# Toeplitz tiles of a state-space mixer laid out on chip by sixteen transfers, in place of a write and a windowed read of memory

## The chip, the cores and the metric

One core of a Trainium2 chip runs the kernel. The metric is the time of one execution on the device in microseconds (us), the median of a few runs. The work of a core is done by TensorE (PE: matmuls), VectorE (DVE), ScalarE (ACT), GpSimd (POOL) and the queue of the sync engine (SP), which issues the transfers. Each engine takes its instructions strictly in the order in which they were written; a semaphore holds an instruction, and with it everything behind it on that engine, until what it needs is there.

## The reference

One layer of a decoder with three groups of heads in parallel: a state-space mixer (S5), differential attention, and sliding-window attention. Sequence 1024, width 1024, float32. What the change touches is the state-space mixer:

```
def s5_mixer(u, lam_re, lam_im, log_step, b_re, b_im, c_re, c_im, d_skip, w_glu, b_glu):
    ...
    bu_re = jnp.einsum('bsgh,gph->bsgp', ug, bb_re)
    bu_im = jnp.einsum('bsgh,gph->bsgp', ug, bb_im)
    ...
    _, _, st_re, st_im = lax.associative_scan(combine, (a_re, a_im, bu_re, bu_im), axis=1)
    y = (jnp.einsum('bsgp,ghp->bsgh', st_re, c_re.astype(jnp.float32))
         - jnp.einsum('bsgp,ghp->bsgh', st_im, c_im.astype(jnp.float32))
         + d_skip.astype(jnp.float32).reshape(SSM_GROUPS, SSM_GROUP) * ug)
    y = jax.nn.gelu(y.reshape(bsz, seq, SSM_WIDTH))
    ...
proj = h @ w_in
(u, z_ssm, qd, kd, vd, z_diff, qs, ks, vs, z_swa) = split_cols(proj)
y_ssm = s5_mixer(u, ...) * jax.nn.silu(z_ssm)
...
y = jnp.concatenate([y_ssm, y_diff, y_swa], axis=-1) @ w_out
return rms_norm(x + gate[:, None, :] * y, final_gain)
```

There are 16 groups of 16 channels with a complex diagonal state of 64 each.

## The kernel before

The projections of the columns of `w_in` (tiles `zu1`, `zs0`, `zs1`, `vs`, `ks`, `qs0`, `qs1`, then `z0`, `v0`, `q0`, `k0`, ...) run one after another on PE. Each weight tile `wr_*` is loaded over the sync queue two tiles ahead (`load_w`, called in `next_w`), split one tile ahead into a high part `wh_*` (a copy on ACT) and a low part `wl_*` (a subtraction on DVE or POOL, `split_w`), and multiplied in three products a step, 24 matmuls for each half `p_*0`, `p_*1` of the sequence. An evacuation then takes the bank: for a query tile, `ev_q` (L1176) writes two pages `qs0m0`, `qs0m1` (or `qs1m*`), their high parts by ACT and their low parts by DVE.

Beside this stream runs the state-space mixer. It works in chunks of eight steps: inside a chunk the convolution is a matmul with a lower-triangular block Toeplitz tile `T`, and between chunks a scan carries the state.

- `ssm_small` (L430) makes `AP`, the powers 0 to 8 of the complex step. `ssm_tables` makes `H`, powers times input weights, and from it, by transposes, `E`.
- `ssm_lags` (L623) makes `CA` and, for the two halves m of the groups, the 16 x 16 blocks of `K` for the eight lags: matmuls into `pK`, two ACT copies, the DVE rows `dd` and `K<-K,dd` for the skip term. `K` has 16 partitions. `T` has 128: row block t holds the lags shifted by t. Before, `K` is written behind seven blocks of zeros (from the page `kz`) into a scratch `kscr` in memory, and one read with overlapping windows lays out the tile: partition block i begins 7 - i blocks from the rear.
- `ssm_main` (L1036) loads `U`, the inputs, with sixteen transfers. Row blocks stand in reversed order, which goes with the reversed rows of `T` and with `AP[..., 0:8]` in `H`.
- `ssm_state(m)` makes the chunk states: matmuls into `pV`, DVE products `tg<-pV,PH`, a sum, a scan, and the result `Xs`.
- `ssm_out(q)` (L1106), q = 0 to 3, is a block of 32 short matmuls on PE into a bank `pY`: `T` times `U` and `CA` times `Xs`. It needs `T`, `Xs` and a free bank of the tag `ps`, of which there are two, shared with `pV`. Its GELU follows on ACT and DVE in the tile `gw`.

Three things set the order around the change. First, a cost model (`Model`, L29 to L94) and a mixer (`Mixer`, L168 to L226): side jobs are generators, and after each step of the projection stream `mix.tick()` writes down the next piece of any job whose inputs the model holds to be ready. So a changed cost or transfer shifts the order in which later instructions stand on all engines. In the model a transfer to 16 partitions takes 0.7 on the sync queue and any other 0.47. Second, all queues are in order. Third, the pages: `page()` (L249) gives every tile one of 50 slots of 4 KB by 128 partitions, in a ring, and a slot passes from a tile that is done to a later one. The first writer of the new tile waits for the last reader of the old one. One page more or fewer early on changes who inherits from whom later.

```
    def page(name, shape=(128, 1024), dt=F32):
        return big.tile(list(shape), dt, name=name, tag="pg", bufs=NPG)
```

All instructions are recorded through one helper, so that every row of the profile says L109; rows are told apart by tile.

Of the kernel before, what the change touches and what calls it, by code (L numbers as in the profile page):

```python
# [8 lines left out]
F32 = mybir.dt.float32  # L9
# [220 lines left out]
def body(ctx, tc, x, c, norm_gain, ada_w, ada_b, w_in, w_out, lam_re, lam_im, log_step,  # L230
# [199 lines left out]
    def ssm_small():  # L430

        M = 12582912.0
        t, kf, r, t2 = small("t_"), small("kf"), small("r_"), small("t2")
        ki = cst.tile([128, 8], I32, name="ki")

        def ts(o, i, s1, o1=OP.mult, s2=None, o2=OP.add):
            if s2 is None:
                V.tensor_scalar(o, i, s1, None, op0=o1)
            else:
                V.tensor_scalar(o, i, s1, s2, op0=o1, op1=o2)  # L440
            return ("V",)

        def tt(o, a, b, op=OP.mult):
            V.tensor_tensor(o, a, b, op)
            return ("V",)

        def stt(o, i, s1, b, o1=OP.mult, o2=OP.add):
            V.scalar_tensor_tensor(o, i, s1, b, op0=o1, op1=o2)
            return ("V",)

        def horner(o, x, ks):

            yield ts(o, x, ks[0])
            for k in ks[1:]:
                yield stt(o, o, k, x, OP.add, OP.mult)

        def exp(o, i):
            yield ts(t, i, -87.0, OP.max, 88.0, OP.min)
            yield ts(kf, t, 1.0 / math.log(2.0))
            yield ts(kf, kf, M, OP.add)  # L460
            yield ts(kf, kf, M, OP.subtract)
            yield stt(r, kf, -0.693359375, t)
            yield stt(r, kf, 2.12194440e-4, r)
            yield from horner(o, r, (1.0 / 5040, 1.0 / 720, 1.0 / 120, 1.0 / 24, 1.0 / 6, 0.5, 1.0))
            ts(kf, kf, 127.0, OP.add, 8388608.0, OP.mult)
            V.tensor_copy(ki, kf)
            yield ("V",)
            yield stt(o, o, 1.0, ki.bitcast(F32), OP.add, OP.mult)

        step, x1, mag, ang = small("step"), small("x1"), small("mag"), small("ang")  # L470
        yield from exp(step, ls)
        tt(x1, lr, step)
        yield tt(ang, li, step)
        yield from exp(mag, x1)
        yield ts(t, ang, 2.0 / math.pi)
        yield ts(kf, t, M, OP.add)
        yield ts(kf, kf, M, OP.subtract)
        yield stt(r, kf, -1.5703125, ang)
        for cc in (-4.837512969970703e-4, -7.549789948768648e-8):
            yield stt(r, kf, cc, r)  # L480
        r2, sn, cs = small("r2"), small("sn"), small("cs")
        yield tt(r2, r, r)
        yield from horner(sn, r2, (1.0 / 362880, -1.0 / 5040, 1.0 / 120, -1.0 / 6))
        yield tt(sn, sn, r)
        yield tt(sn, sn, r, OP.add)
        yield from horner(cs, r2, (-1.0 / 3628800, 1.0 / 40320, -1.0 / 720, 1.0 / 24, -0.5))
        yield ts(cs, cs, 1.0, OP.add)
        f1, b0, b1 = small("f1"), small("b0"), small("b1")
        for q, i, b in ((f1, kf, b0), (t, f1, b1)):

            yield ts(q, i, 0.5, OP.mult, -0.25)
            yield ts(q, q, M, OP.add)
            yield ts(q, q, M, OP.subtract)
            yield stt(b, q, -2.0, i)
        yield ts(b1, b1, -2.0, OP.mult, 1.0)
        e = cst.tile([128, 2, 8], F32, name="e")
        yield tt(t2, cs, sn, OP.subtract)
        yield tt(t2, t2, b0)
        yield tt(t2, t2, sn, OP.add)
        yield tt(e[:, 1], t2, b1)  # L500
        yield tt(t2, cs, sn, OP.add)
        yield tt(t2, t2, b0)
        yield tt(t2, cs, t2, OP.subtract)
        yield tt(e[:, 0], t2, b1)
        PW["e"] = e

        AP = page("AP", (128, 2, 8, 9))
        G.memset(AP[:, 0, :, 0:1], 1.0)
        G.memset(AP[:, 1, :, 0:1], 0.0)
        yield tt(AP[:, :, :, 1], e, mag[:, None, :].to_broadcast([128, 2, 8]))  # L510
        pt = page("pt_", (128, 4, 8, 4))
        for n in (1, 2, 4):
            src = [AP[:, u, :, 1:n + 1] for u in range(2)]
            bc = [AP[:, u, :, n:n + 1].to_broadcast([128, 8, n]) for u in range(2)]
            q = [pt[:, j, :, :n] for j in range(4)]
            tt(q[0], src[0], bc[0])
            tt(q[1], src[1], bc[1])
            yield tt(q[2], src[0], bc[1])
            tt(q[3], src[1], bc[0])
            tt(AP[:, 0, :, n + 1:2 * n + 1], q[0], q[1], OP.subtract)  # L520
            yield tt(AP[:, 1, :, n + 1:2 * n + 1], q[2], q[3], OP.add)
        fre, fim, am, t3 = small("fre"), small("fim"), small("am"), small("t3")
        yield ts(am, AP[:, 0, :, 1], 1.0, OP.subtract)
        tt(t2, AP[:, 1, :, 1], li)
        yield tt(fre, am, lr)
        tt(t3, am, li)
        yield tt(fim, AP[:, 1, :, 1], lr)
        tt(fre, fre, t2, OP.add)
        yield tt(fim, fim, t3, OP.subtract)
        tt(fre, fre, den)  # L530
        yield tt(fim, fim, den)
        M8 = small("M8")
        yield tt(M8, mag, mag)
        yield tt(M8, M8, M8)
        yield tt(M8, M8, M8)
        PW.update(AP=AP, M8=M8, fre=fre, fim=fim)

    def ssm_phases():

# [20 lines left out]
    def ssm_tables():  # L560

        yield from ssm_small()
        yield (when(lambda: "B" in PW),)
        AP, fre, fim = PW["AP"], PW["fre"], PW["fim"]
        t0 = page("tb0", (128, 8, 8, 16))
        t1 = page("tb1", (128, 8, 8, 16))
        fb = [f[:, :, None].to_broadcast([128, 8, 16]) for f in (fre, fim)]
        v0, v1 = t0[:, :, 0, :], t1[:, :, 0, :]
        for u in range(2):
            tts(v0, Bq[:, u], fb[0], OP.mult)  # L570
            tts(v1, Bq[:, 1 - u], fb[1], OP.mult)
            tts(BB[:, u], v0, v1, OP.add if u else OP.subtract)
            yield ("V",)
        for u in range(2):
            for g2 in range(2):
                V.tensor_copy(BS[RH[u], :, g2], BB[RH[g2], u])
        mix.add(ssm_lags())
        H = [page(f"H{u}", (128, 8, 8, 16)) for u in range(2)]
        av = [AP[:, u, :, 0:8][:, :, :, None].to_broadcast([128, 8, 8, 16]) for u in range(2)]
        bv = [BB[:, u][:, :, None, :].to_broadcast([128, 8, 8, 16]) for u in range(2)]  # L580
        for u in range(2):
            tts(t0, av[0], bv[u], OP.mult)
            yield ("V",)
            tts(t1, av[1], bv[1 - u], OP.mult)
            yield ("V",)
            tts(H[u], t0, t1, OP.add if u else OP.subtract)
            yield ("V",)

        E = [page(f"E{u}", (128, 8, 128)) for u in range(2)]
        PW["E"] = E  # L590
        for u in range(2):
            for m in range(2):
                yield (H[u], bank("pt"))
                p = pst("pt", "pE", (128, 4, 128))
                for a in range(4):
                    PE.transpose(p[:, a], H[u][:, 4 * m + a].rearrange("p a b -> p (a b)"), ident)
                A.activation(E[u][:, 4 * m:4 * m + 4], p, AF.Copy)
                rel(p)
# [19 lines left out]
                yield (c_,)  # L618
        PW["ph"] = 1

    kscr = [dram.tile([16, 8, 15, 16], F32, name=f"kscr{m}") for m in range(2)]

    def ssm_lags():  # L623
        kz = page("kz", (16, 8, 7, 16))
        G.memset(kz, 0.0)
        for m in range(2):
            SP.dma_start(kscr[m][:, :, 0:7, :], kz)
        yield (Cn, bank("pt"))
        psc = pst("pt", "psc", (128, 2, 128))
        for u in range(2):  # L630
# [32 lines left out]
        rel(pd)  # L663
        Tm = [page(f"T{m}", (128, 8, 8, 16)) for m in range(2)]
        for m in range(2):
            K = page(f"K{m}", (16, 8, 8, 16))
            for g2 in range(2):
                yield (CA[m][g2], BS, bank("pt"))
                p = pst("pt", "pK", (16, 4, 128))
                for a in range(4):  # L670
# [6 lines left out]
            tts(dd, ident[:16, None, :16].to_broadcast([16, 8, 16]),  # L677
                dT[:, 8 * m:8 * m + 8, None].to_broadcast([16, 8, 16]), OP.mult)
            tts(K[:, :, 0, :], K[:, :, 0, :], dd, OP.add)

            SP.dma_start(kscr[m][:, :, 7:15, :], K)
            SP.dma_start(Tm[m].rearrange("p a b c -> p a (b c)"),
                         dap(kscr[m], 0, [[16, 8], [15 * 128, 16], [15 * 16, 8], [1, 128]]))
        PW["T"] = Tm


# [349 lines left out]
    def ssm_main():  # L1036
        Uu = []
        for f in range(2):
            t = page(f"U{f}", (128, 8, 128))
            for tt in range(8):  # L1040
                SP.dma_start(t[112 - tt * 16:128 - tt * 16], dap(uscr, f * 128 * 1024 + tt * 128,
                                                           [[1024, 16], [16 * 1024, 8], [1, 128]]))
            Uu.append(t)
        yield (when(lambda: "ph" in PW and "E" in PW),)
# [633 lines left out]
```

## Time and profile before

| | |
|---|---|
| median of three runs | 572.88 us (569.91 to 575.13) |
| profiled execution | 573.08 us |
| its span, first to last instruction | 571.3 us |
| mean granted clock of PE | 0.991 |
| busy time of PE | 553.9 us of the span |

A row of the timeline gives the start in us, the duration, the engine, the operation, output and inputs with their shapes, how many such instructions are joined, and in brackets how long the engine stood idle before and what released it. A row of the windows gives a stretch, its length, the busy time of PE, of PE's weight loads, DVE, ACT and POOL with their counts, then the clock that PE was granted (1.00 is full), the share of the transfer engines that was busy and GB/s. A row of the waits gives engine and tile, what it waited for, us in total, times and the longest.

### The profile page before, as it was taken

To read this page: it belongs to the slowest core of one execution; us is meant where nothing else is said; L and a number is where in the kernel's file an instruction comes from. 1 tells how busy PE (TensorE), PEld (TensorE's weight loads), DVE (VectorE), ACT (ScalarE), POOL (GpSimd) and SP (SyncE) were. 2 spreads that over 40 slices of the span, in tenths; PEclk is the share of its full clock that TensorE was granted. 3 is DMA by queue.
4 is the path that set the end of the run, shared out by engine and by line. 5 is a ranking of instruction groups with operands and counts; after the bars stand their busy time and mean duration, and the time that the engine had idled before them with its cause. 6 is when DMAs were issued, how large, how long until landed. Compare 5 with 4: busy or idle time off the path is not lost.

```text
span 571.3 us, 9236 instructions
## 1 busy us (share of the span) xinstructions
PE 553.9 (97%) x3170; PEld 464.3 (81%) x3170; DVE 403.8 (71%) x1061; ACT 262.3 (46%) x595; POOL 188.3 (33%) x339
## 2 busy tenths in 40 slices
PE   8999999999997999999999999999999999989995
PEld 6767888888887996777888889998888878878884
DVE  4886886997687666788666777744766867765534
ACT  6545221255142545435555766535575456442211
POOL 3254170000135036442646172323453522120011
PEclk9999999999998999999999999999999999989998
DMA  8993076002712430437320111015026402051411
GB/s 315 353 349 71 3 202 138 0 2 47 148 37 52 86 105 38 176 130 230 103 73 2 38 37 38 2 34 188 2 75 215 154 1 65 0 178 64 139 38 73
DMA packets 60634, 57.12 MB, mean 100 GB/s; under 512 B 11375, under 2 KB 52906, under 8 KB 60586
## 3 DMA queue, kind: packets, MB, share of 16 engines
q1 hardware_dynamic: 60518, 56.50, 32.9%
q8 instruction: 25, 0.41, 0.3%
q14 instruction: 23, 0.19, 0.1%
q10 hardware_dynamic: 68, 0.02, 0.0%
HBM read 46.83 MB, written 9.68 MB: 99 GB/s over the span
## 4 chain that ended last, share of the span: by engine, by line
PE 86%; DVE 9%; ACT 2%; issue 2%; POOLq 0%; POOL 0%; DVEq 0%; ACTq 0%
PE po L109 14%; PE pb L109 10%; PE p_v L109 7%; PE p_k L109 6%; PE p_z L109 6%; PE pS L109 6%; PE pdO L109 6%; PE p_q L109 5%; PE p_zs L109 4%; PE p_qs L109 3%; PE pdT L109 2%; PE p_ks L109 2%; PE p_vs L109 2%; PE p_zu L109 2%; PE pa L109 2%
## 5 line engine op out<-in xcount | busy, mean ns | idle before, releaser
L109 ACT ACTIVATE sp<-sp,dmx 128x128 f32<-128x128 f32 (+7 forms) x64 | 49.0, 768 | 18.4 <-DVE dmx L109 18.3
L109 PE MATMUL po<-woh,yh 128*128 128x512 f32 (+1 forms) x136 | 52.3, 384 | 0.1
L109 PE MATMUL po<-woh,yl 128*128 128x512 f32 (+1 forms) x136 | 51.6, 379 | 0.3 <-DVE yl L109 0.3
L109 PE MATMUL po<-wol,yh 128*128 128x512 f32 (+1 forms) x136 | 51.4, 378 | 0.0
L109 POOL TENSOR_SCALAR dmx<-dmx 128x1 f32<-128x1 f32 x32 | 6.5, 204 | 112.0 <-ACT oo L109 111.2
L109 DVE CUSTOM_DVE_ANT_0 sp<-pS,bd 128x384 f32<-128x384 f32 (+3 forms) x64 | 33.8, 552 | 10.3 <-PE pS L109 9.6
L109 PE MATMUL p_v<-wh_v,hh 128*128 128x256 f32 x128 | 37.8, 295 | 0.0
L109 PE MATMUL p_v<-wl_v,hh 128*128 128x256 f32 x128 | 36.4, 285 | 1.0 <-POOL wl_v L109 1.0
L109 PE MATMUL p_v<-wh_v,hl 128*128 128x256 f32 x128 | 36.2, 283 | 0.0
L109 POOL TENSOR_TENSOR swp<-swp,swm 128x256 f32<-128x256 f32 x30 | 19.9, 696 | 41.0 <-DVE swm L109 31.9
L109 PEld LDWEIGHTS po<-woh,yl 128*128 128x128 f32 x136 | 25.6, 188 | 5.5 <-DVE yl L109 0.7
L109 PEld LDWEIGHTS po<-woh,yh 128*128 128x128 f32 x136 | 25.8, 189 | 4.6 <-ACT yh L109 0.3
L109 ACT ACTIVATE jk<-res 128x512 f32<-128x512 f32 (+1 forms) x16 | 9.8, 616 | 42.3 <-DVE res L109 42.3
L109 PEld LDWEIGHTS po<-wol,yh 128*128 128x128 f32 x136 | 25.7, 189 | 4.2
L109 POOL TENSOR_TENSOR wl_z<-wr_z,wh_z 128x256 fp32r<-128x256 f32 x16 | 12.6, 818 | 44.7 <-ACT wh_z L109 44.7
L109 PE MATMUL p_k<-hh,wh_k 128*128 128x512 f32 x64 | 26.3, 411 | 0.0
L109 PE MATMUL p_q<-hh,wh_q 128*128 128x512 f32 x64 | 26.1, 407 | 0.0
L109 PEld LDWEIGHTS p_v<-wl_v,hh 128*128 128x128 f32 x128 | 24.4, 191 | 1.9 <-POOL wl_v L109 1.4
L109 PE MATMUL p_z<-hh,wh_z 128*128 128x512 f32 x64 | 25.5, 398 | 0.0
L109 PEld LDWEIGHTS p_v<-wh_v,hh 128*128 128x128 f32 x128 | 24.4, 190 | 0.9 <-issue 0.8
L109 PE MATMUL p_q<-hh,wl_q 128*128 128x512 f32 x64 | 25.1, 393 | 0.0
L109 PE MATMUL p_k<-hh,wl_k 128*128 128x512 f32 x64 | 25.1, 393 | 0.0
(486 smaller groups left out, 1673.9 us busy)
## 6 DMA issues: line engine op xcount, KB each, us to landing
aw<-in_ada_w_dram SPq DMA_DIRECT2D x32, 256.0 KB
x<-in_x_dram SPq DMA_DIRECT2D x8, 512.0 KB
gaw<-in_ada_w_dram SPq DMA_DIRECT2D x8, 512.0 KB
wo<-in_w_out_dram SPq DMA_DIRECT2D x8, 512.0 KB
xr<-in_x_dram SPq DMA_DIRECT2D x8, 512.0 KB
out_dram<-res SPq DMA_DIRECT2D x16, 256.0 KB
yt<-ycat SPq DMA_DIRECT2D x48, 64.0 KB
wr_z<-in_w_in_dram SPq DMA_DIRECT2D x4, 512.0 KB
```

Source lines behind the costliest of these rows:

```text
L109: return f(*args, **kw)
```

## The change

Four edits go together.

1. A new page `ARV` holds `AP` in reversed order of the powers, made by eight copies on POOL, and `H` is made from `ARV`. 
2. The scratch `kscr`, the page `kz`, its memset and its two transfers are gone.
3. `T` is set to zero on POOL, two memsets of 1024 elements a partition, and each half m is then laid out by eight transfers from `K` in place: the t-th writes the 16 partitions of row block t with the lags 0 to 7 - t, for 8 groups: for t = 0 a run of 4 KB in each partition, else 8 runs of 448 down to 64 bytes.
4. `U` is loaded with its row blocks in natural order.

```diff
--- before.py
+++ after.py
@@ -519,6 +519,9 @@
             tt(q[3], src[1], bc[0])
             tt(AP[:, 0, :, n + 1:2 * n + 1], q[0], q[1], OP.subtract)
             yield tt(AP[:, 1, :, n + 1:2 * n + 1], q[2], q[3], OP.add)
+        ARV = page("ARV", (128, 2, 8, 8))
+        for j in range(8):
+            G.tensor_copy(ARV[:, :, :, j], AP[:, :, :, 7 - j])
         fre, fim, am, t3 = small("fre"), small("fim"), small("am"), small("t3")
         yield ts(am, AP[:, 0, :, 1], 1.0, OP.subtract)
         tt(t2, AP[:, 1, :, 1], li)
@@ -533,7 +536,7 @@
         yield tt(M8, mag, mag)
         yield tt(M8, M8, M8)
         yield tt(M8, M8, M8)
-        PW.update(AP=AP, M8=M8, fre=fre, fim=fim)
+        PW.update(AP=AP, ARV=ARV, M8=M8, fre=fre, fim=fim)
 
     def ssm_phases():
 
@@ -561,7 +564,7 @@
 
         yield from ssm_small()
         yield (when(lambda: "B" in PW),)
-        AP, fre, fim = PW["AP"], PW["fre"], PW["fim"]
+        ARV, fre, fim = PW["ARV"], PW["fre"], PW["fim"]
         t0 = page("tb0", (128, 8, 8, 16))
         t1 = page("tb1", (128, 8, 8, 16))
         fb = [f[:, :, None].to_broadcast([128, 8, 16]) for f in (fre, fim)]
@@ -576,7 +579,7 @@
                 V.tensor_copy(BS[RH[u], :, g2], BB[RH[g2], u])
         mix.add(ssm_lags())
         H = [page(f"H{u}", (128, 8, 8, 16)) for u in range(2)]
-        av = [AP[:, u, :, 0:8][:, :, :, None].to_broadcast([128, 8, 8, 16]) for u in range(2)]
+        av = [ARV[:, u][:, :, :, None].to_broadcast([128, 8, 8, 16]) for u in range(2)]
         bv = [BB[:, u][:, :, None, :].to_broadcast([128, 8, 8, 16]) for u in range(2)]
         for u in range(2):
             tts(t0, av[0], bv[u], OP.mult)
@@ -618,13 +621,7 @@
                 yield (c_,)
         PW["ph"] = 1
 
-    kscr = [dram.tile([16, 8, 15, 16], F32, name=f"kscr{m}") for m in range(2)]
-
     def ssm_lags():
-        kz = page("kz", (16, 8, 7, 16))
-        G.memset(kz, 0.0)
-        for m in range(2):
-            SP.dma_start(kscr[m][:, :, 0:7, :], kz)
         yield (Cn, bank("pt"))
         psc = pst("pt", "psc", (128, 2, 128))
         for u in range(2):
@@ -663,6 +660,7 @@
         rel(pd)
         Tm = [page(f"T{m}", (128, 8, 8, 16)) for m in range(2)]
         for m in range(2):
+            G.memset(Tm[m], 0.0)
             K = page(f"K{m}", (16, 8, 8, 16))
             for g2 in range(2):
                 yield (CA[m][g2], BS, bank("pt"))
@@ -677,10 +675,8 @@
             tts(dd, ident[:16, None, :16].to_broadcast([16, 8, 16]),
                 dT[:, 8 * m:8 * m + 8, None].to_broadcast([16, 8, 16]), OP.mult)
             tts(K[:, :, 0, :], K[:, :, 0, :], dd, OP.add)
-
-            SP.dma_start(kscr[m][:, :, 7:15, :], K)
-            SP.dma_start(Tm[m].rearrange("p a b c -> p a (b c)"),
-                         dap(kscr[m], 0, [[16, 8], [15 * 128, 16], [15 * 16, 8], [1, 128]]))
+            for t in range(8):
+                SP.dma_start(Tm[m][t * 16:t * 16 + 16, :, t:8, :], K[:, :, 0:8 - t, :])
         PW["T"] = Tm
 
 
@@ -1038,7 +1034,7 @@
         for f in range(2):
             t = page(f"U{f}", (128, 8, 128))
             for tt in range(8):
-                SP.dma_start(t[112 - tt * 16:128 - tt * 16], dap(uscr, f * 128 * 1024 + tt * 128,
+                SP.dma_start(t[tt * 16:(tt + 1) * 16], dap(uscr, f * 128 * 1024 + tt * 128,
                                                            [[1024, 16], [16 * 1024, 8], [1, 128]]))
             Uu.append(t)
         yield (when(lambda: "ph" in PW and "E" in PW),)
```

The sync queue holds ten instructions more. These are the rows of it around the change, on both sides (the shape behind the names is that of the output, the brackets hold the semaphores waited for). Before:

```order
L109 DMA kscr0_151<-K0_1421 128x1x128 [waits DVE_49]
L109 DMA T0_1419<-kscr0_151 128x8x128 [waits DMAHW5_49,DMAHW3_49,DMAHW6_49,DMAHW2_49,DMAHW1_49]
L109 DMA kscr1_152<-K1_1473 128x1x128 [waits DVE_49]
L109 DMA T1_1420<-kscr1_152 128x8x128 [waits DMAHW4_49,DMAHW3_49,PE_49]
L109 DMA wr_z0_1517<-in_w_in_dram 128x8x128 [waits PE_49]
L109 DMA wr_v0_1589<-in_w_in_dram 128x4x256
```

Now:

```order
L109 DMA T0_1428<-K0_1431 16x8x16 [waits DMAHW6_49]
L109 DMA T1_1429<-K1_1469 16x1024 [waits DMAHW7_49,DVE_49,Pool_49]
L109 DMA T1_1429<-K1_1469 16x8x112 [waits DMAHW0_49]
L109 DMA T1_1429<-K1_1469 16x8x96 [waits DMAHW1_49]
L109 DMA T1_1429<-K1_1469 16x8x80 [waits DMAHW2_49]
L109 DMA T1_1429<-K1_1469 16x8x64 [waits DMAHW3_49]
L109 DMA T1_1429<-K1_1469 16x8x48 [waits DMAHW4_49]
L109 DMA T1_1429<-K1_1469 16x8x32 [waits DMAHW5_49]
L109 DMA T1_1429<-K1_1469 16x8x16 [waits DMAHW6_49]
L109 DMA wr_z0_1534<-in_w_in_dram 128x8x128 [waits DMAHW7_49,PE_49]
L109 DMA wr_v0_1606<-in_w_in_dram 128x4x256 [waits DMAHW0_49,PE_49]
```

The eight transfers of `T0` stand ahead of those shown of `T1`; the weights `wr_z0` and `wr_v0` follow behind in both. `wr_v0` now waits for PE, for the end of `p_qs01`.

On ACT these are the rows between the split of `qs1` and the first evacuation of `pY` (`p_qs00` and `p_qs01` are the two halves of the product with `qs0`, `p_qs10` the first of `qs1`). Before:

```order
L109 ACTIVATE wh_qs1_1519<-wr_qs1_1344 128x1024 [waits DMAHW7_49,DMAHW0_49]
L109 ACTIVATE qs0m0_1515<-p_qs00_1523 64x512 [waits PE_49]
L109 ACTIVATE qs0m1_1516<-p_qs00_1523 64x512
L109 ACTIVATE qs0m0_1515<-p_qs01_1552 64x512 [waits PE_49]
L109 ACTIVATE qs0m1_1516<-p_qs01_1552 64x512
L109 ACTIVATE wh_z0_1593<-wr_z0_1517 128x1024 [waits DMAHW5_49]
L109 ACTIVATE qs1m0_1587<-p_qs10_1600 64x512 [waits PE_49,Activation_49,Pool_49]
```

Now:

```order
L109 ACTIVATE wh_qs1_1536<-wr_qs1_1322 128x1024 [waits DMAHW6_49,DMAHW5_49]
L109 ACTIVATE qs0m0_1532<-p_qs00_1540 64x512 [waits PE_49]
L109 ACTIVATE qs0m1_1533<-p_qs00_1540 64x512 [waits PE_49]
L109 ACTIVATE qs0m0_1532<-p_qs01_1569 64x512 [waits PE_49]
L109 ACTIVATE qs0m1_1533<-p_qs01_1569 64x512
L109 ACTIVATE wh_z0_1610<-wr_z0_1534 128x1024 [waits DMAHW4_49,DMAHW5_49,DMAHW3_49,DMAHW6_49,DMAHW2_49,DMAHW7_49,DMAHW1_49,DMAHW0_49]
L109 ACTIVATE qs1m0_1604<-p_qs10_1617 64x512 [waits PE_49,Activation_49,Pool_49]
```

They stand in the same order. The third row, the second evacuation of `p_qs00`, now has a wait for PE: its page `qs0m1` was held by `wl_ks` before and is now held by `wh_qs0`, which the products of `p_qs01` read; the wait is for the last of these, PE's second-to-last matmul of `p_qs01`. The split of `z0` waits for eight semaphores, which cover its page's earlier use.

On DVE these rows follow the last low parts of `qs0` (`tg0`, `tg1` are the products of `ssm_state` for m = 1; the row on `M8` and `tg` is the scan). Before:

```order
L109 TENSOR_TENSOR tg0_1466<-pV1_1456,PH1_975 128x512
L109 TENSOR_TENSOR tg1_1467<-pV0_1447,PH1_975 128x512
L109 TENSOR_TENSOR qs1m0_1587<-p_qs10_1600,qs1m0_1587 64x512 [waits PE_49,DMAHW5_49,Activation_49,Pool_49]
L109 TENSOR_TENSOR qs1m1_1588<-p_qs10_1600,qs1m1_1588 64x512 [waits DVE_49]
L109 TENSOR_TENSOR tg0_1466<-tg0_1466 128x512 [waits DVE_49]
L109 SCALAR_TENSOR_TENSOR tg0_1466<-M8_1103,tg0_1466 128x128 [waits DVE_49]
L109 SCALAR_TENSOR_TENSOR tg0_1466<-M8_1103,tg0_1466 128x128 x3
L109 TENSOR_TENSOR tg1_1467<-tg1_1467 128x512
L109 SCALAR_TENSOR_TENSOR tg1_1467<-M8_1103,tg1_1467 128x128 [waits DVE_49]
L109 SCALAR_TENSOR_TENSOR tg1_1467<-M8_1103,tg1_1467 128x128 x3
```

Now:

```order
L109 TENSOR_TENSOR tg0_1506<-pV1_1496,PH1_973 128x512
L109 TENSOR_TENSOR tg1_1507<-pV0_1487,PH1_973 128x512
L109 TENSOR_TENSOR tg0_1506<-tg0_1506 128x512 [waits DVE_49]
L109 SCALAR_TENSOR_TENSOR tg0_1506<-M8_1101,tg0_1506 128x128 [waits DVE_49]
L109 SCALAR_TENSOR_TENSOR tg0_1506<-M8_1101,tg0_1506 128x128 x3
L109 TENSOR_TENSOR qs1m0_1604<-p_qs10_1617,qs1m0_1604 64x512 [waits PE_49,DMAHW7_49,Activation_49,Pool_49]
L109 TENSOR_TENSOR qs1m1_1605<-p_qs10_1617,qs1m1_1605 64x512
L109 TENSOR_TENSOR tg1_1507<-tg1_1507 128x512
L109 SCALAR_TENSOR_TENSOR tg1_1507<-M8_1101,tg1_1507 128x128 [waits DVE_49]
L109 SCALAR_TENSOR_TENSOR tg1_1507<-M8_1101,tg1_1507 128x128 x3
```

One sum and its scan, those of `tg0`, now stand ahead of the low parts of `qs1`. On PE the first block of `pY` stands directly behind the last matmul of `p_qs10`, where before three matmuls of `p_qs11` came first.

## The prediction

> **What bounds the kernel now.** I read the page's first part and its chain first, then the waits of PE alone, then the stretch from 130 to 190 us engine by engine.
>
> ```profile
> PE 553.9 (97%) x3170; PEld 464.3 (81%) x3170; DVE 403.8 (71%) x1061; ACT 262.3 (46%) x595; POOL 188.3 (33%) x339
> PE 86%; DVE 9%; ACT 2%; issue 2%; POOLq 0%; POOL 0%; DVEq 0%; ACTq 0%
> ```
>
> TensorE (PE) is busy for 97% of the span. No transfer ends the chain of waits, so an edit of transfers counts only where it lets PE stop, or keeps it from stopping. The waits of PE show where it stops; the columns are us in total, times, longest.
>
> ```profile
> PE pY L109 <- DVE gw L109: 2.4, 1, 2.4
> PE p_v L109 <- POOL wl_v L109: 1.0, 2, 0.5
> ```
>
> Both lie in the stretch that the change touches. PE's rows there (start, us, tile, what ended the idle time):
>
> ```profile
> 146.37 0.39 PE L109 MATMUL p_qs<-hl,wh_qs 128*128 128x512 f32 x1
> 152.95 0.38 PE L109 MATMUL pY<-U,T 128*128 128x128 f32 x2
> 156.43 0.48 PE L109 MATMUL p_qs<-hh,wh_qs 128*128 128x512 f32 x1
> 161.29 0.39 PE L109 MATMUL p_z<-hh,wh_z 128*128 128x512 f32 x1
> 174.44 0.28 PE L109 MATMUL p_v<-wh_v,hh 128*128 128x256 f32 x1
> 175.23 0.39 PE L109 MATMUL p_v<-wl_v,hh 128*128 128x256 f32 x1 [0.51 <-POOL wl_v L109]
> 178.61 0.28 PE L109 MATMUL p_v<-wl_v,hh 128*128 128x256 f32 x1
> 178.73 0.28 PE L109 MATMUL p_v<-wh_v,hl 128*128 128x256 f32 x1
> 181.37 0.49 PE L109 MATMUL pY<-U,T 128*128 128x128 f32 x2 [2.36 <-DVE gw L109]
> 186.59 0.36 PE L109 MATMUL p_v<-wh_v,hh 128*128 128x256 f32 x1
> 182.00:184.00 2.00, 2.00 (x11) 2.00 (x11) 0.10 (x1) 0.00 (x0) 0.00 (x0) 0.50 0.40 72
> 505.93 0.30 PE L109 MATMUL pdy<-ident,do 128*128 128x128 f32 x1 [1.72 <-DVE do L109]
> 506.00:508.00 2.00, 2.00 (x11) 2.00 (x12) 2.00 (x6) 0.00 (x0) 0.00 (x0) 0.53 0.53 141
> ```
>
> A block of pY, 32 matmuls, takes 156.43 - 152.95 = 3.48 us the first time and 186.59 - 181.37 = 5.22 us the second time. The rows that begin with two times are windows, and the number before the last two is the granted clock: 0.50 after the 2.36 us gap, 0.53 after the 1.72 us gap at 505.93. So a gap of that size costs its length and 5.22 - 3.48 = 1.74 us besides. The pace of p_v is 178.73 - 178.61 = 0.12 us a matmul, so PE could have begun pY at 178.85; the gap itself is 181.37 - 178.85 = 2.52 us, and each of the two waits for wl_v costs 175.23 - 174.44 - 0.12 = 0.67 us. Removable in this stretch: 2.52 + 1.74 + 2 x 0.67 = 5.6 us.
>
> Why is gw late? Follow it back through VectorE (DVE), ScalarE (ACT), GpSimd (POOL) and the sync queue:
>
> ```profile
> 142.82 1.39 DVE L109 TENSOR_TENSOR qs0m<-p_qs,qs0m 64x512 fp32r<-64x512 f32 x2 [0.50 <-ACT qs0m L109]
> 151.08 1.29 DVE L109 TENSOR_TENSOR tg<-pV,PH 128x512 f32<-128x512 f32 x2
> 158.66 1.41 DVE L109 TENSOR_TENSOR qs1m<-p_qs,qs1m 64x512 fp32r<-64x512 f32 x2 [6.29 <-ACT qs1m L109]
> 160.82 1.37 DVE L109 TENSOR_TENSOR_SCAN tg<-M,tg 128x128 f32<-128x128 f32 x4
> 171.97 0.69 DVE L109 SCALAR_TENSOR_TENSOR z<-z,p_z 128x512 f32<-128x512 f32 x1
> ```
> ```profile
> 141.58 1.20 ACT L109 ACTIVATE qs0m<-p_qs 64x512 fp32r<-64x512 f32 x2 [0.52 <-PE p_qs L109]
> 147.02 1.20 ACT L109 ACTIVATE qs0m<-p_qs 64x512 fp32r<-64x512 f32 x2 [4.24 <-PE p_qs L109]
> 153.33 1.06 ACT L109 ACTIVATE wh_z<-wr_z 128x1024 fp32r<-128x1024 f32 x1 [5.11 <-DMA wr_z<-in_w_in_dram]
> 157.35 1.21 ACT L109 ACTIVATE qs1m<-p_qs 64x512 fp32r<-64x512 f32 x2 [2.96 <-POOL wl_z L109]
> 162.71 2.01 ACT L109 ACTIVATE wh_v<-wr_v 128x1024 fp32r<-128x1024 f32 x2
> 154.52 2.80 POOL L109 TENSOR_TENSOR wl_z<-wr_z,wh_z 128x256 fp32r<-128x256 f32 x4 [34.69 <-ACT wh_z L109]
> 163.86 4.27 POOL L109 TENSOR_TENSOR wl_v<-wr_v,wh_v 128x256 fp32r<-128x256 f32 x4 [6.23 <-ACT wh_v L109]
> ```
> ```profile
> 73.31 9.78 SPq L109 DMA_DIRECT2D U<-uscr  x16
> 132.52 0.56 SPq L109 DMA_DIRECT2D kscr<-K  x1
> 135.04 0.63 SPq L109 DMA_DIRECT2D T<-kscr  x1
> 142.85 0.62 SPq L109 DMA_DIRECT2D T<-kscr  x1
> 143.51 1.64 SPq L109 DMA_DIRECT2D wr_z<-in_w_in_dram  x1
> 145.20 4.20 SPq L109 DMA_DIRECT2D wr_v<-in_w_in_dram  x2
> ```
>
> The read of T1 is issued at 142.85, wr_z behind it, and wr_z is there only at 153.33. ACT's wh_z and POOL's wl_z (done at 157.3) hold ACT's qs1m to 157.35, and DVE stands for 6.29 us. After that DVE has no gap until gw, and PE gets there first.
>
> **The change, part by part.** *Removed:* one memset (kz, row below), two writes of zeros, two writes of K, two reads of 512 KB. *Added and hidden on POOL:* eight copies for ARV and two memsets of T.
>
> ```profile
> 72.17 0.33 POOL L109 COPY PH<-UK 128x8 f32<-128x8 f32 x2 [12.42 <-issue]
> 83.13 0.84 POOL L109 MEMSET kz<- 16x896 f32 x1
> 119.72 0.11 POOL L109 MEMSET Xs<- 128x8 f32 x1 [34.00 <-PE pv L109]
> ```
>
> A copy of 128x16 by two rows of 128x8: 8 x 0.33 = 2.6 us at most, behind AP at 85.6. A memset of 1024 elements by the kz row: 0.84 x 1024/896 = 0.96 us, two of them near 119. POOL rests for 34.00 us ahead of the third row, and H, T and U are needed tens of us later. Without that cover they would cost 4.5 us. H reading ARV and U written in natural order change no count: nothing.
>
> *The sixteen transfers.* The nearest row is U<-uscr: the same kind, 16 partitions and up to eight runs each, 16 issued in 9.78 us, so 0.61 us each. K0's first write is issued at 132.52 today; the DVE rows ahead of it are as many, in another order, for which I allow one pair of tg (1.29 us, the 151.08 row): 133.8. Sixteen issues end at 133.8 + 9.8 = 143.6, the moment at which wr_z is issued now. But most of T1 has moved by then instead of being about to start, and the two wr_v now wait for the end of PE's p_qs (about 147), so wr_z moves alone. It lands between 143.6 + 2.5 = 146.1 (the kscr write was answered within 135.04 - 132.52 = 2.52 us) and 143.6 + 9.8 = 153.4 (as today, with T1's read ahead and wr_v beside it). I take 147, near the first, as nothing shares the queue. Even the second end costs nothing in what follows, which needs wh_z at 153.4 at the earliest.
>
> So far this is a gain: wl_z would be done by 152.5, the qs1m wait would go, and the 5.6 us with it.
>
> *The new wait.* The pages form a ring of 50. With ARV in it and kz out of it, qs0m1 gets the page that held wh_qs0. In the order, ACT's second evacuation of p_qs00 therefore carries a wait for PE that was not there. It is for the last reader of wh_qs0: PE's second-to-last matmul of p_qs01, the 146.37 row, whose result is signalled about 0.45 us later (146.8). Today that evacuation ends with the 141.58 row, at 142.78. ACT is in order, and DVE's first subtraction waits for both evacuations. Its start moves from 142.82 to 146.8 + 0.6 + 0.1 = 147.5, so 4.68 us later, and the run of DVE rows behind it, which has no gap down to tg<-pV at 151.08, moves as a whole. Queued behind are Xs0 and the tg<-pV that frees a bank for pY; PE's pY needs both. The first half of that pair, the last reader of the bank, ends at about 151.08 + 1.29/2 = 151.7 today; 4.68 later it is 156.4, and PE starts at about 156.45.
>
> *What PE does.* In the order, pY stands three p_qs matmuls earlier: 152.95 - 3 x 0.227 = 152.27 (29 matmuls from the 146.37 row to 152.95, so 0.227 each). It stops there until 156.45: 4.18 us. The clock then falls as it did at 181.37: 1.74 us. PE leaves this place 5.9 us later.
>
> *What comes next.* DVE's order has the add and scan of tg ahead of qs1m (0.69 + 1.37 = 2.06 us), so qs1m starts at 157.05 + 2.06 = 159.1 (the tg pair ends at 152.37 + 4.68), close to 158.66. Then p_qs11 ends at 161.3 + 5.9 = 167.2, POOL's wl_v follows 163.86 - 161.29 = 2.57 us behind, as today (ACT's qs1m and half of wh_v lie between), at 169.8, and ends 4.27 later at 174.1; ACT evacuates z in 0.6 (its page is wr_v's, which wl_v reads) and DVE's z starts at 174.7 instead of 171.97: 2.73 us later. From z to gw DVE is saturated, so pY's release moves from 181.37 to 184.1. PE arrives at 178.85 - 1.34 (no waits for wl_v left: PE is 5.9 later, wl_v 1.8) + 5.9 = 183.4. It waits 0.7 us. That is too short to lower the clock if the next two rows hold: a gap of 1.01 us left it at 1.00.
>
> ```profile
> 461.98 0.52 PE L109 MATMUL pdT<-ident,sp 128*128 128x128 f32 x3 [1.01 <-DVE sp L109]
> 462.00:464.00 2.00, 1.64 (x7) 0.92 (x8) 1.42 (x4) 1.12 (x3) 1.43 (x3) 1.00 0.00 0
> ```
>
> The block at full clock ends at 184.1 + 3.48 = 187.6, against 186.59. Sum: +1.0 us (+4.18 + 1.74 + 0.7 - 5.6 = +1.0). Bounds: without a fall of the clock at the first stall, -0.7; with one at the second as well, +2.7. Behind 190 us both orders name the same waits, so the shift is kept to the end: span 571.3 + 1.0 = 572.3. The profiled execution took 573.08, 1.78 around its span: 574.1; it lies 0.2 above the median 572.88, so 573.9 us.
>
> The Trainium skill ("TensorE: Matmul & The Clock Gate", "What's actually happening") lets the clock halve after an idle window of about 3.4 us. By that, the 2.36 us gap would not be what halved the clock; the 1.74 us would stay in the second pY, and the sum would be +2.7. The rows at 181.37 and 505.93 speak against it: two gaps under 3.4 us, each with a clock near 0.5 behind it. I keep +1.0.
>
> **Rivals.**
>
> *A, the gain comes through:* the slot wait is met early enough to be harmless, T no longer holds wr_z, and the 5.6 us go: 567.3. For it: the DVE gap of 6.29 us is real and the queue is freed. Against: the matmul that must be waited for has a row, 146.37, and PE runs without a gap up to it. 0.11.
>
> *B, slower:* the sixteen transfers move one after another, each at the 2.52 us of the kscr write. T0 would be complete at 133.8 + 20.2 = 154 (before pY starts), T1 at 174, and wr_z behind it at about 177; wh_z at 178.1, so p_z, which PE would reach at 167.2, begins at 178.1: 16.8 after today's 161.29. Less the 5.6 that go, plus a clock fall of 1.74: +12.9, 586. It decides from the pace at which wr_z lands after 158: DVE's z at 174.7 needs qs1m by 163.5, wh_z by 158.3, wr_z's last byte then, T's end near 155, that is 1.3 us each, twice the 0.61 of U's row. That row, of the same shape, speaks against it. 0.07.
>
> The Trainium skill speaks for it ("DMA: Bandwidth & Descriptors", "Rules for kernel authors"): small transfers should be joined, since under 64 KB one pays mostly overhead. No row here shows runs of 64 B.
>
> *C, nothing moves:* the wait and the freed queue balance or both stay under cover: 572.9 within the spread of the runs (569.91 to 575.13). 0.17.
>
> *The forecast:* 0.65, by itself 571.0 to 576.8 (572.2 and 575.6 from the two bounds, with a share of the runs' spread).
>
> **How the numbers follow.** One per cent, about what a measurement of this kernel tells from no change, is 567.2 to 578.6. Faster takes most of A and none of the rest, 0.08; slower takes B and the tail of the forecast with two clock falls, 0.09; the rest is 0.83. The range goes from 568.0, into the gain of A, to 578.0; B is left out.
>
> **What would show it.** Right: ACT's second qs0m ends its wait on PE near 146.8; DVE qs0m at 147.5; wr_z there before 150, no 6.3 us DVE gap before qs1m; a stop of about 4 us before the first pY with a clock of 0.5 behind it; no wait for wl_v; the second pY gap under 1 us at full clock. Wrong: the first pY not held, or wh_z waiting on wr_z beyond 155, or PE waiting anywhere behind 190 us where it does not now.

## The result and the profile after

| | median, us | ratio to before, 95% interval |
|---|---|---|
| before (14 runs) | 572.84 | |
| changed (14 runs) | 575.66 | 1.0052 (1.0033 to 1.0071) |

The changed kernel is slower by half a per cent, 1.9 to 4.1 us. The forecast was 573.9 us and no change within 1%. The profiled execution took 575.75 us with a span of 574.0, the one of before 573.08 with 571.3.

The five largest waits of PE in the changed kernel, over the whole span (us in total, times, longest):

```profile
PE pY L109 <- issue: 5.4, 1, 5.4
PE pdT L109 <- DVE sp L109: 2.0, 3, 1.0
PE pdy L109 <- DVE do L109: 1.9, 2, 1.7
PE pb L109 <- DVE two L109: 1.6, 1, 1.6
PE pb L109 <- ACT xt L109: 1.0, 1, 1.0
```

Rows two to four are as before or within 0.1 us of it. The waits for wl_v and the wait of pY for gw are gone. In their place stands one stop before a pY block, of 5.4 us; "issue" means that the profile names no releaser for it. The last row is a late start at 15 us: it appears in some traces and not in others (the experiments below show 0 to 1.3 us of it, with the same instructions there), so 1.0 us is taken off the times of this trace wherever they are held against before.

PE at the place, in the changed kernel's timeline:

```profile
153.05 0.39 PE L109 MATMUL p_qs<-hh,wl_qs 128*128 128x512 f32 x1
158.89 0.76 PE L109 MATMUL pY<-U,T 128*128 128x128 f32 x2 [5.44 <-issue]
164.56 0.48 PE L109 MATMUL p_qs<-hh,wh_qs 128*128 128x512 f32 x1
186.03 0.39 PE L109 MATMUL pY<-U,T 128*128 128x128 f32 x2
189.53 0.36 PE L109 MATMUL p_v<-wh_v,hh 128*128 128x256 f32 x1
```

PE could have begun pY at 153.05 + 0.23 = 153.28 and began at 158.89: 5.6 us. The block then takes 164.56 - 158.89 = 5.67 us where a full clock gives 3.48. The second pY follows without a gap and takes 189.53 - 186.03 = 3.50 us. The windows show the clock (the third number from the right):

```profile
154.00:156.00 2.00, 0.00 (x0) 0.00 (x0) 1.95 (x4) 0.14 (x1) 1.83 (x2) 1.00 0.00 1
156.00:158.00 2.00, 0.00 (x0) 0.00 (x0) 1.97 (x3) 0.45 (x1) 0.00 (x0) 0.62 0.00 0
158.00:160.00 2.00, 1.11 (x5) 1.14 (x6) 1.95 (x4) 0.59 (x1) 0.00 (x0) 0.50 0.00 0
160.00:162.00 2.00, 2.00 (x11) 2.00 (x10) 1.98 (x5) 0.00 (x0) 0.00 (x0) 0.50 0.00 0
162.00:164.00 2.00, 2.00 (x14) 2.00 (x14) 1.92 (x5) 0.60 (x1) 0.00 (x0) 0.67 0.00 0
```

PE stands still, DVE is busy for 1.95 us or more of every 2, and the clock falls to 0.50 during the stop. DVE is what PE waits for: the first half of its pair tg<-pV (fifth DVE row below), which gives a bank back, ends at about 158.09 + 1.29/2 = 158.7, and pY begins at 158.89. The experiment "wl_z later" tests this. ACT, DVE, POOL and the sync queue of the changed kernel:

```profile
142.60 0.59 ACT L109 ACTIVATE qs0m<-p_qs 64x512 fp32r<-64x512 f32 x1 [0.54 <-PE p_qs L109]
147.81 1.82 ACT L109 ACTIVATE qs0m<-p_qs 64x512 fp32r<-64x512 f32 x3 [4.62 <-PE p_qs L109]
150.33 1.06 ACT L109 ACTIVATE wh_z<-wr_z 128x1024 fp32r<-128x1024 f32 x1 [0.70 <-DMA wr_z<-in_w_in_dram]
```
```profile
148.44 1.39 DVE L109 TENSOR_TENSOR qs0m<-p_qs,qs0m 64x512 fp32r<-64x512 f32 x2 [5.12 <-ACT qs0m L109]
149.84 1.28 DVE L109 TENSOR_TENSOR tg<-tg,PH 128x508 f32<-128x508 f32 x2
151.16 1.82 DVE L109 TENSOR_TENSOR Xs<-tg,tg 64x508 f32<-64x508 f32 x2
153.00 2.25 DVE L109 TENSOR_TENSOR tg<-tg,PH 128x508 f32<-128x508 f32 x2
158.09 1.29 DVE L109 TENSOR_TENSOR tg<-pV,PH 128x512 f32<-128x512 f32 x2
176.68 0.69 DVE L109 SCALAR_TENSOR_TENSOR z<-z,p_z 128x512 f32<-128x512 f32 x1
```
```profile
151.47 4.36 POOL L109 TENSOR_TENSOR wl_z<-wr_z,wh_z 128x256 fp32r<-128x256 f32 x4 [20.07 <-ACT wh_z L109]
135.17 10.71 SPq L109 DMA_DIRECT2D T<-K  x16
145.98 0.54 SPq L109 DMA_DIRECT2D wr_z<-in_w_in_dram  x1
```

One ACT row has become two: the first evacuation of p_qs00 at 142.60 stands alone (x1), the second is held 4.62 us by PE and joins the pair of p_qs01 (x3). DVE's qs0m waits 5.12 us with it. The freed queue did what it was to do: wr_z is there at 150.33, and the 6.29 us gap of DVE before its first qs1m rows is gone.

### The profile page after: what moved, and what is told of

Same layout as the page of the kernel before. It is cut to its first block, busy times and chain, and to the rows that moved or that the text cites. A ratio compares the mean times of both kernels' runs of the same rounds, so it can differ in the third digit from the quotient of the medians.

```text
span 574.0 us, 9267 instructions
## 1 busy us (share of the span) xinstructions
PE 553.7 (96%) x3170; PEld 464.1 (81%) x3170; DVE 404.0 (70%) x1061; ACT 262.0 (46%) x595; POOL 191.5 (33%) x348
## 4 chain that ended last, share of the span: by engine, by line
PE 86%; DVE 5%; DMA 3%; ACT 2%; issue 2%; POOL 1%; SPq 0%; POOLq 0%; DVEq 0%; ACTq 0%
PE po L109 14%; PE pb L109 8%; PE p_z L109 8%; PE p_v L109 7%; PE p_k L109 7%; PE pS L109 6%; PE pdO L109 5%; PE p_q L109 5%; PE p_zs L109 4%; PE p_qs L109 3%; PE pdT L109 2%; DMA x<-in_x_dram 2%; PE p_ks L109 2%; PE p_vs L109 2%; PE p_zu L109 2%
## 5 line engine op out<-in xcount | busy, mean ns | idle before, releaser
L109 PE MATMUL p_q<-hl,wh_q 128*128 128x512 f32 x64 | 25.1, 392 | 0.0
L109 PE MATMUL p_z<-hh,wl_z 128*128 128x512 f32 x64 | 25.0, 391 | 0.0
```

What stands on the lines that cost most here:

```text
L109: return f(*args, **kw)
```

## The experiments

Eight kernels, in two groups; each group shares its runs of the kernel before (medians 571.30 and 571.16 us). A time is the median of a kernel's runs; a ratio is an estimate over all runs with its 95% interval, and can differ by about 0.1% from the quotient of the two medians.

**One page for K.** Both halves of K share one page, on partitions 0 to 15 and 64 to 79, so one page more is free when qs0's pages are handed out. The cost model is told the two halves apart, as it was with two pages, so every engine's order stays that of the changed kernel.

```diff
         Tm = [page(f"T{m}", (128, 8, 8, 16)) for m in range(2)]
+        KK = page("KK", (80, 8, 8, 16))
         for m in range(2):
             G.memset(Tm[m], 0.0)
-            K = page(f"K{m}", (16, 8, 8, 16))
+            h = slice(64 * m, 64 * m + 16)
+            K = KK[h]
...
-            dd = sml.tile([16, 8, 16], F32, name="dd", bufs=1)
+            dd = sml.tile([80, 8, 16], F32, name="dd", bufs=1)[h]
```

> The changed kernel with both halves of K on one page (partitions 0 to 15 and 64 to 79), so that one page is free earlier; every engine has its instructions in the same order, and of the waits near the place only that of ACT's second qs0m evacuation on PE's p_qs01 is gone. Theory S (the slot wait is the cost): ACT evacuates both pages of p_qs00 together at about 142.6, DVE's qs0m starts near 143.8 instead of 148.4, PE's stop of 5.4 us before the first pY shrinks to at most 0.8 us and the clock stays at 1.00; the gain that the freed queue brings comes through, no wait for wl_v and none or a short one before the second pY: 567.2 to 568.5 us, ratio to before 0.990 to 0.993. Rival Q (the sixteen transfers, or the order that they bring, cost the time): no better than the changed kernel, 575 to 576 us, ratio 1.004 to 1.006.

Measured: 566.53 us, ratio 0.9918 (0.9902 to 0.9933). The rows of ACT, DVE and PE:

```profile
141.37 1.20 ACT L109 ACTIVATE qs0m<-p_qs 64x512 fp32r<-64x512 f32 x2 [0.54 <-PE p_qs L109]
142.60 1.39 DVE L109 TENSOR_TENSOR qs0m<-p_qs,qs0m 64x512 fp32r<-64x512 f32 x2 [0.51 <-ACT qs0m L109]
149.44 1.82 DVE L109 TENSOR_TENSOR Xs<-tg,tg 64x508 f32<-64x508 f32 x2
151.29 1.29 DVE L109 TENSOR_TENSOR tg<-pV,PH 128x512 f32<-128x512 f32 x2
152.09 0.46 PE L109 MATMUL pY<-U,T 128*128 128x128 f32 x2
177.13 0.39 PE L109 MATMUL pY<-U,T 128*128 128x128 f32 x2
```

ACT takes both pages at once again (x2), DVE's qs0m starts at 142.60, neither pY row has idle time ahead of it, and PE has no wait between 130 and 200 us. Of the waits near the place only the slot wait was removed (1.0052 became 0.9918), and 1.3% went with it; what is left, 0.8% faster than before, is the gain of the freed queue. Rival Q falls.

**The transfers alone.** The kernel before with the sixteen transfers, T's row blocks in reversed order, U and H untouched, no ARV.

```diff
-        kz = page("kz", (16, 8, 7, 16))
-        G.memset(kz, 0.0)
...
+            G.memset(Tm[m], 0.0)
...
+            for t in range(8):
+                SP.dma_start(Tm[m][112 - t * 16:128 - t * 16, :, t:8, :], K[:, :, 0:8 - t, :])
```

> The kernel before with the sixteen transfers alone: T is written with its row blocks in reversed order, U and H stay as they were, no ARV page and no copies on POOL. Theory K (K's pages are held longer, by eight transfers where one write was, and that is what hands wh_qs0's page to qs0m1): the wait of ACT on PE and the stop before pY are there as in the changed kernel, ratio 1.003 to 1.007. Rival, as the prediction had it (ARV's page in place of kz moves the pages): the stop is gone, 567 to 570 us, ratio below 0.996.

Measured: 573.12 us, ratio 1.0039 (1.0023 to 1.0055).

```profile
142.87 0.59 ACT L109 ACTIVATE qs0m<-p_qs 64x512 fp32r<-64x512 f32 x1 [0.53 <-PE p_qs L109]
148.09 1.81 ACT L109 ACTIVATE qs0m<-p_qs 64x512 fp32r<-64x512 f32 x3 [4.62 <-PE p_qs L109]
159.63 0.77 PE L109 MATMUL pY<-U,T 128*128 128x128 f32 x2 [4.55 <-issue]
```

The split pair (x1, x3) and the stop are there without ARV. The slot wait comes with this edit, which replaces kz and the way through memory by the transfers and the memsets of T.

**wl_z later.** In the changed kernel, POOL's four wl_z subtractions are held until DVE has made the last product tg<-pV of the second half.

```diff
         rel(*vp)
+        if m and "late" in PW:
+            ...
+            nc.gpsimd.tensor_copy(PW["sq"][:, 0, 0:1], t3[:, 0, 0:1])
+            for c in range(0, 1024, 256):
+                nc.gpsimd.tensor_sub(lo_[:, c:c + 256], raw_[:, c:c + 256], hi_[:, c:c + 256])
```

> The changed kernel with POOL's four wl_z subtractions held until DVE has made the last tg<-pV product of the second half (one tiny copy on POOL reads it first). Theory P (DVE's Xs and tg rows between 151 and 155.3 took 4.07 us instead of 2.65 because POOL's wl_z ran beside them): these rows take 1.28 to 1.38 us again, the stop before the first pY falls from 5.4 to about 4.1 us, 574.3 us, ratio 1.0025. Rival (their length has another cause): the stop stays at 5.4 us, ratio 1.005.

Measured: 573.30 us, ratio 1.0035 (1.0023 to 1.0048).

```profile
PE pY L109 <- issue: 4.0, 1, 4.0
150.10 1.38 DVE L109 TENSOR_TENSOR Xs<-tg,tg 64x508 f32<-64x508 f32 x2
151.49 1.28 DVE L109 TENSOR_TENSOR tg<-tg,PH 128x508 f32<-128x508 f32 x2
157.54 3.38 DVE L109 TENSOR_TENSOR_SCAN tg<-M,tg 128x128 f32<-128x128 f32 x4
157.51 3.13 POOL L1088 TENSOR_TENSOR wl_z<-wr_z,wh_z 128x256 fp32r<-128x256 f32 x4
```

The two DVE rows are back at 1.38 and 1.28 us, and the stop is 1.4 us shorter. The length moved with POOL's rows: now the scan beside them takes 3.38 us instead of 1.37. The ratio went from 1.0052 to 1.0035, about 1.0 us, but the two intervals overlap: the rows and the stop show the effect, the times do not.

**Both edits.**

> Both edits of the two kernels above (one page for K, wl_z later). Theory S with P: no stop before the first pY at all, up to 0.8 us better than one page for K alone, 567 to 568 us, ratio 0.990 to 0.992. Rival Q: 575 us.

Measured: 566.12 us, ratio 0.9912 (0.9897 to 0.9927), which is not told apart from one page for K alone. PE has no wait left between 130 and 200 us that a faster DVE could shorten.

**The transfers alone, with one page for K.** The edits of the first two kernels together.

> The kernel before with the sixteen transfers alone (no ARV, U and H as before) and both halves of K on one page. Theory S: without the slot wait the transfers bring their gain whatever the row order of T: no stop of 4 us before the first pY, 566 to 568.5 us, ratio 0.990 to 0.994. Rival R (the gain of one page for K needed the scan of tg ahead of qs1m, or ARV): 570 us or more, ratio above 0.996.

Measured: 565.68 us, ratio 0.9918 (0.9893 to 0.9942), and no wait of PE between 130 and 200 us. ARV and the row order bring nothing of their own that can be told, and rival R falls.

**The copies alone.** The kernel before with the ARV page and its copies, which nothing reads.

```diff
+        ARV = page("ARV", (128, 2, 8, 8))
+        for j in range(8):
+            nc.gpsimd.tensor_copy(ARV[:, :, :, j], AP[:, :, :, 7 - j])
```

> The kernel before with the ARV page and its eight copies on POOL alone (nothing reads them). Hidden on an idle POOL: no change, ratio 0.998 to 1.002, eight copies within 2.6 us on POOL, no new stop of PE. Rival (the page or the copies move something): a new wait of PE and a ratio beyond 1.002.

Measured: 571.0 us, ratio 1.0000 (0.9978 to 1.0022).

```profile
84.74 1.26 POOL L524 COPY ARV<-AP 128x16 f32<-128x16 f32 x8 [5.07 <-DVE AP L109]
```

Eight copies take 1.26 us together on an idle engine.

**Each transfer twice.** In the changed kernel, and in the one with one page for K.

```diff
             for t in range(8):
                 SP.dma_start(Tm[m][t * 16:t * 16 + 16, :, t:8, :], K[:, :, 0:8 - t, :])
+            for t in range(8):
+                nc.sync.dma_start(Tm[m][t * 16:t * 16 + 16, :, t:8, :], K[:, :, 0:8 - t, :])
```

> The changed kernel with each of the sixteen transfers issued twice (the second set writes the same values). Theory S with slack: wr_z is issued near 156.7 instead of 146.0 and wl_z runs behind the DVE rows, so the first stop shrinks by about 1.4 us to 4.0, and the late qs1m gives 0.3 to 3.4 us back before the second pY: 575 to 578 us, ratio 1.004 to 1.010. Rival Q (the transfers' 10.7 us on the queue are on the path): 10 us more than the changed kernel, 585 us, ratio 1.024.

Measured: 573.20 us, ratio 1.0039 (1.0021 to 1.0058): 10 us more on the queue cost nothing that can be told against the changed kernel's 1.0052, and rival Q with its 1.024 falls here too. The profile has the wait for the page and a late wr_z beside each other:

```profile
147.48 1.39 DVE L109 TENSOR_TENSOR qs0m<-p_qs,qs0m 64x512 fp32r<-64x512 f32 x2 [5.11 <-ACT qs0m L109]
164.47 1.39 DVE L109 TENSOR_TENSOR qs1m<-p_qs,qs1m 64x512 fp32r<-64x512 f32 x2 [5.46 <-ACT qs1m L109]
159.22 1.06 ACT L109 ACTIVATE wh_z<-wr_z 128x1024 fp32r<-128x1024 f32 x1 [10.55 <-DMA wr_z<-in_w_in_dram]
```

ACT waits 10.55 us for wr_z and DVE 5.46 us behind it, yet between 130 and 200 us PE's only stop is the first one, of 4.0 us. As wl_z now runs behind the DVE rows, this stop is the shorter one of "wl_z later"; and as PE is held by it, it comes to p_v only at 179 us, when DVE's late qs1m is done. The ratio is just under the expected 1.004 to 1.010; I had allowed for a second stop, which did not come.

> One page for K and each of the sixteen transfers issued twice. Here nothing hides a late wr_z: issued near 155.2 instead of 144.7, wh_z near 159.5, wl_z done near 163.5, PE's third p_z matmul (161.7) held for about 2 us, qs1m on DVE near 165 instead of 155, and a stop before the second pY as in the kernel before or longer, with the clock halved: 574 to 578 us, ratio 1.004 to 1.012, so the whole gain is gone. If the place in the queue does not matter: 566.5 us, ratio 0.992.

With one page for K, measured: 575.32 us, ratio 1.0073 (1.0050 to 1.0097).

```profile
PE p_v L109 <- DVE qs1m L109: 2.2, 1, 2.2
PE p_v L109 <- POOL wl_v L109: 1.3, 3, 0.5
PE pY L109 <- DVE gw L109: 0.8, 1, 0.8
164.63 1.39 DVE L109 TENSOR_TENSOR qs1m<-p_qs,qs1m 64x512 fp32r<-64x512 f32 x2 [10.85 <-ACT qs1m L109]
```

Without the slot wait the same 10 us are on the path: the ratio goes from 0.9918 with one page for K alone to 1.0073. The size was as expected and the place was not: I named p_z's third matmul and a longer stop before the second pY; PE stopped at p_v instead, which needs the bank that the late qs1m gives back. The granted clock fell twice behind these stops, to 0.51 at 174 us and to 0.50 at 182.

## Why the prediction was right, and where it was off

*The total.* The forecast of no change within 1% holds, and so does the range. Its size does not: the sum was +1.0 us, and the measured 1.9 to 4.1 us leave that out, while the upper bound, +2.7, lies inside. That the error stayed small was in part luck, because misses of both signs cancel: the first stop and the clock cost 1.9 us more than reckoned, the second stop 0.7 us less, and the cause given for the new wait was wrong although the wait itself was read rightly from the order.

*The gain.* "Removable in this stretch: 5.6 us" by a freed queue. One page for K measures it: a ratio of 0.9918 on 571.30 is 4.7 us less (3.8 to 5.6), and the 5.6 lie at the edge of that interval. wr_z was there by 150.33, 149.3 on the time of before, instead of the 147 that I took and inside the bounds of 146.1 and 153.4. The sixteen issues took 10.71 us where U's row gave 9.8.

*The new wait.* The place, the row and the start of DVE's qs0m are as predicted: 148.44 less the late start of 1.0 is 147.4, predicted 147.5. Its cause was not. "With ARV in it and kz out of it, qs0m1 gets the page that held wh_qs0": the copies and their page move nothing, and the transfers without ARV bring the wait. The order of before hands K0's page, free after one write to memory, to wl_qs1; in the changed one K0 serves eight transfers, wl_qs1 takes a page of the ks weights, and qs0m1 is left with that of wh_qs0. That one page more undoes it is shown; that K's longer hold is what took it is read from the order and fits both runs, but no run changed the hold alone: the transfers-alone kernel also leaves out kz and writes T's pages earlier, by its memsets. The orders of kernels that were built and not run speak for the hold: with only the memsets added, with only kz left out, or with both, qs0m1 takes a page of the ks weights as before; with the transfers and no memsets it takes that of wh_qs0.

*The first stop, 4.18 us predicted, 5.6 us measured: the term that was mis-sized.* I moved a run of seven DVE rows "as a whole" at its old lengths. But wl_z, no longer late, now ran on POOL beside it, and two rows took 1.82 + 2.25 instead of 1.38 + 1.28 us: 1.41 us, which is the whole difference between 4.18 and 5.6. Holding wl_z back returned them and 1.4 us of the stop. The trace of before had a row for it, which I did not weigh: the same product takes 1.28 us at 144.24 and 2.31 us at 164.10, with POOL's wl_v at 163.86 beside it.

```profile
144.24 1.28 DVE L109 TENSOR_TENSOR tg<-tg,PH 128x508 f32<-128x508 f32 x2
164.10 2.31 DVE L109 TENSOR_TENSOR tg<-tg,PH 128x508 f32<-128x508 f32 x2
```

The Trainium skill has this rule ("GPSIMD Engine Reference", "1. Specifications": GpSimd shares its interfaces to on-chip memory with VectorE, and they contend where the VectorE instruction has two inputs from there or runs in a 2-port mode). The traces agree for the two inputs: tg<-tg,PH and the scan lengthen, while tg<-pV,PH, one of whose inputs is a PSUM bank, takes 1.29 us in the one-page kernel with wl_z beside it. No run here tests the 2-port mode.

*The clock:* 1.74 us predicted, 5.67 - 3.48 = 2.2 measured. The second block ran at full clock, in 3.50 us, as predicted; the larger sum of +2.7, in which it stays slow, did not come.

*What comes next.* z starts at 176.68, 175.7 on the time of before, predicted 174.7: the first stop and the slow clock were longer by 1.9 us, and wl_v gave some of it back with 3.02 us instead of 4.27. A little of this was lost again on a path that I had left out: z also stands behind DVE's rows jm and bsw, and with wl_v beside them they took 1.24 + 2.41 us where before they took 0.36 + 1.43. They end at 174.24 + 2.41 = 176.65, after ACT's evacuation of z (175.84 + 0.60). The second pY: 0.7 us of wait predicted, none measured. The two gw rows ahead of it took 0.42 us each, not 0.97 and 0.92 as before, which made up for the later z. The rows, of the changed kernel and then of before:

```profile
172.68 3.02 POOL L109 TENSOR_TENSOR wl_v<-wr_v,wh_v 128x256 fp32r<-128x256 f32 x4 [7.67 <-ACT wh_v L109]
183.50 0.42 DVE L109 TENSOR_SCALAR gw<-gw 128x512 f32<-128x512 f32 x1
```
```profile
179.08 0.92 DVE L109 TENSOR_SCALAR gw<-gw 128x512 f32<-128x512 f32 x1
```

Why the gw rows were shorter is open; POOL's wl_q alone does not explain it, since it ran beside both rows of before (176.27 to 179.72) but also beside the second of the changed kernel (182.82 to 185.92), which took 0.42 us. The block ends at 189.53 - 1.0 = 188.5, against 186.59: +1.9 us in this trace where +1.0 was predicted. The 14 runs say +1.9 to +4.1, so this place explains the measured loss at its lower edge; the rest is not settled.

*The rivals.* A, the gain coming through, needed the slot wait to be harmless; it is the 0.9918 of the one-page kernels, 4.7 us where 5.6 was worked out. B, a slow pace of the transfers, falls with the changed kernel's own trace: wr_z was there by 150.33 and not at 177. The two doubled kernels add that at twice the queue time a loss does appear, but only where no slot wait covers it. C, nothing moves, falls with the interval of 1.0033 to 1.0071, though the gain of the freed queue, 0.8%, does cancel most of the 1.3% that the slot wait costs.

## What to carry to other kernels

A tile that is read by more transfers than before is given back later, and in a pool without a spare slot another tile's first writer can pay for it, on an engine that the edit does not name: look for waits that are new in the order before pricing the transfers. When a stage is moved in time, price its rows beside what will run then, not beside what ran before. A gain and a new wait on the same path can hide each other; take one of them out before dropping the change, as one page for K turned 0.5% slower into 0.8% faster.

## What the runs showed of the hardware

The same stop of PE does not always cost the same. The stop of 1.72 us before pdy is in every trace; the clock fell behind it at 506 us in the kernel before and did not fall in the changed one, whose fall came instead at 467, behind a stop of 1.01 us that left the clock of before at 1.00. Windows of the kernel before, then rows and windows of the changed one:

```profile
506.00:508.00 2.00, 2.00 (x11) 2.00 (x12) 2.00 (x6) 0.00 (x0) 0.00 (x0) 0.53 0.53 141
```
```profile
464.84 0.52 PE L109 MATMUL pdT<-ident,sp 128*128 128x128 f32 x3 [1.01 <-DVE sp L109]
468.00:470.00 2.00, 2.00 (x11) 1.90 (x10) 0.91 (x3) 0.56 (x2) 0.00 (x0) 0.50 0.00 0
510.38 0.30 PE L109 MATMUL pdy<-ident,do 128*128 128x128 f32 x1 [1.72 <-DVE do L109]
510.00:512.00 2.00, 1.62 (x15) 1.65 (x16) 2.00 (x7) 0.00 (x0) 0.00 (x0) 1.00 0.54 148
```

Of the ten profiled executions, one of each kernel, five had a fall behind pdy and five had none. Such a fall is worth about 1.7 us (an estimate from the two windows behind 506 us, at 0.53 and 0.61). Executions of one kernel differ in their clock too: of the 23 of the kernel before in the second group, the fastest, 567.91 us, had a mean granted clock of 0.998, and the slowest, 573.03 us, one of 0.990. The rule that I drew from two rows, that a gap of 1.7 to 2.4 us halves the clock and one of 1.01 does not, was too firm. The Trainium skill ("TensorE: Matmul & The Clock Gate", "What's actually happening") has the clock judged in windows of 3.4 us that run freely. That fits with stops of one length that count in one execution and not in another; its threshold of a whole idle window does not, since stops of 1.01 and 1.72 us were enough here.
